# Three re-orderings in a hybrid diffusion trunk: the opening's products, weight cuts in the norm between layers, a convolution chunk

## The chip, the cores and the metric

The kernel runs on one core of one Trainium2 chip. The metric is the device time of one execution in microseconds (us); before the change it was 1175.28 (median of 3 runs, 1175.14 to 1176.17). The engines go by their names in the profile: PE (TensorE, matrix products; PEld its weight loads), DVE (VectorE), ACT (ScalarE), POOL (GpSimd), SP (SyncE, which issues most DMAs). Each runs its instructions in the order in which the program lists them, and waits for the others by semaphores.

## What is computed

Two layers over 512 tokens of width 1024, with a context of 256 tokens:

```python
for l in range(DEPTH):                                  # DEPTH = 2
    m = (sc_c @ w_mod[l] + b_mod[l])[:, None, :]        # sc_c = silu(c)
    sh1, s1, g1, sh2, s2, g2 = jnp.split(m, 6, axis=-1)
    h = modulate(rmsnorm(x, norm_g[l, 0]), sh1, s1)     # h * (1 + scale) + shift
    if l % 2 == 0:      # spatial gating beside neighbourhood attention
        hc = modulate(rmsnorm(ctx, norm_g[l, 0]), csh1, cs1)
        y, yc = even_mixer(h, hc, w_in[i], w_out[i], ...)
    else:               # gated projection, 31-tap convolution, layer norm, silu, projection
        y = conformer_conv(h, w_pw1[i], b_pw1[i], w_dw[i], ...)
    x = x + g1 * y
    x = x + g2 * sq_relu_mlp(modulate(rmsnorm(x, norm_g[l, 1]), sh2, s2), w_ff1[l], w_ff2[l])
return rmsnorm(x, final_g)
```

All is in float32.

## The kernel before

Activations lie transposed: channels on the 128 partitions, in 8 blocks k, tokens along the free axis (two halves of 256, a and b). A product in float32 accuracy is made of three matmuls: each operand is split into a high part (a cast, ACT, L93) and a low part (a subtraction on DVE or POOL, L94), and `mm3` (L88 to L90) issues high x high, weight's low x high, and high x operand's low. In `first_products` these are called hh, lh and hl. The order is written out by hand: the scheduler is off, every engine runs what the Python code emits, in that order.

Weights come in tiles of 1 MB (`raw`, two buffers) and are cut in four *pieces* each (`W.piece(i, q)`: cast on ACT, subtraction on DVE, or on POOL with `pool`, or on both by turns with "both"). The last piece of a tile issues the DMA of a later one. `W.pieces(n)` cuts the next n pieces where it stands in the code.

**Opening.** The first norm's factor: squares and sums (L383 to L393) give `dev`, `deviations()` (L405, four small products and a copy) spreads it to `r0`, `scaled(f)` multiplies two blocks of x by it. The modulation of layer 0 is made in four parts f: `mod_products(f)` (L421, twice four matmuls of 32 columns of weights `wmA`), a copy (ACT, L426), `next`, four transposes (L430), `next`, and three small DVE operations to shift and scale (L435 to L438). Then `first_operand(f)` makes the operand blocks k = 2f and 2f + 1 (hhi on ACT, L464; hlo on DVE, L465 and L466). `first_products(ks, ns)` multiplies them into four banks `q0`, of two weight tiles (n = 0, 1 and 2, 3). After f = 3 follow: a weight cut with POOL, the last first products (k = 6, 7), squares and additions over the context (ACT and DVE, L310 to L321), and their column sum on PE (`total`, L327).

**Norm between layers.** `norm_between` is called three times: ahead of layer 0's MLP (near 260 us), ahead of the convolution (610) and ahead of layer 1's MLP (800). It ends one projection and begins the next without a gap: output blocks 4 and 5 whole (`chunk`), 6 and 7 for token half a, then for half b. `residual`'s evacuation adds a block into x (DVE, L1012), squares it (ACT, L313) and adds the square *of the block before* (DVE, L321; `flush` adds the last one). `ss.total(a0, a1)` (flush, then L327) stands inside the products of block 6, half b; from it ACT and DVE make the factor (L331, L332), and `modulate`, one step of the generator for each k, makes t (DVE, L346), hhi (ACT) and hlo (DVE for even, POOL for odd k, one step later). The next layer's four products for half a (`together(four, ...)`) use these operands k by k; inside them stands the column sum of half b (L327 again).

**Convolution.** `glu(c)` makes the gated block c, and its evacuation (DVE, L1218) writes the padded row `ypad`; SP then issues DMAs that spread it into `y4` (16; for c = 7 only 10, the rest are ACT copies). `conv_pe(c, t0, t1)` runs the taps as 32-column matmuls on `y4` (L1262).

## Time and profile before

| | us |
|---|---|
| median of 3 runs | 1175.28 |
| profiled execution, its own time | 1176.03 |
| its span, first to last instruction | 1174.2 |
| PE busy (share of the span) | 1154.7 (98%) |
| DVE busy | 722.4 (62%) |
| ACT busy | 473.9 (40%) |
| POOL busy | 170.0 (14%) |

The profile's mean granted clock of PE is 0.996 of full speed. PE's busy time is near the whole span, so the places to read are those few where PE waited, which engine it waited for, and how near to waiting it was at the others.

### The profile page before, as it was taken

How to read it: one execution, taken by the hardware profiler on the slowest of the kernel's cores; microseconds unless marked ns; L12 is line 12 of the kernel's file. 1: busy time of each engine (PE TensorE's matmuls, PEld its weight loads, DVE VectorE, ACT ScalarE, POOL GpSimd, SP SyncE). 2: the span in 40 equal slices, each digit the busy share in tenths (PEclk: the TensorE clock that was granted, in tenths of full speed). 3: DMA queues.
4: the chain of work that ended last, by engine and by line, in shares of the span. 5: the costliest groups of instructions: out<-in, count | busy, mean ns of one | idle time of the engine just before them, and what ended most of it. 6: DMA issues, size and time to landing. Idle time of an engine off the chain costs nothing.

```text
span 1174.2 us, 16562 instructions
## 1 busy us (share of the span) xinstructions
PE 1154.7 (98%) x6620; PEld 959.6 (82%) x6620; DVE 722.4 (62%) x1252; ACT 473.9 (40%) x939; POOL 170.0 (14%) x162
## 2 busy tenths in 40 slices
PE   8999999999999999999999999999999999999997
PEld 4688898889888888888889666698988888888887
DVE  4765778758765665666666878577643443443445
ACT  4474455546431422423336233564632331341423
POOL 0250327533000000000023110143200000000001
PEclk9999999999999999999999999999999999999999
DMA  9624543351554554554541444303232332232322
GB/s 383 228 81 137 188 162 109 126 215 37 215 210 152 212 215 156 203 215 172 186 144 41 151 113 140 99 24 122 72 107 73 108 108 77 103 108 72 108 73 72
DMA packets 31469, 161.91 MB, mean 138 GB/s; under 512 B 4320, under 2 KB 7904, under 8 KB 15008
## 3 DMA queue, kind: packets, MB, share of 16 engines
q1 hardware_dynamic: 27360, 146.09, 35.6%
q10 hardware_dynamic: 4032, 14.76, 3.7%
q8 instruction: 52, 0.85, 0.3%
q14 instruction: 25, 0.20, 0.1%
HBM read 152.52 MB, written 2.10 MB: 132 GB/s over the span
## 4 chain that ended last, share of the span: by engine, by line
PE 87%; DVE 6%; DMA 3%; ACT 2%; issue 1%; POOL 0%; ACTq 0%; DVEq 0%; SPq 0%; POOLq 0%
PE ps L88 23%; PE ps L90 22%; PE ps L89 22%; PE ps L214 4%; PE ps L211 4%; PE ps L212 4%; PE ps L1262 3%; PE ps L892 1%; DMA graw<-in_wmA_dram 1%; DVE graw L557 1%; DMA graw<-in_wmB_dram 1%; PE ps L846 1%; DVE acc L321 1%; PE ps L421 1%; PE ps L876 1%
## 5 line engine op out<-in xcount | busy, mean ns | idle before, releaser
L93 ACT CAST whi<-raw 128x512 fp32r<-128x512 f32 x340 | 191.2, 616 | 199.4 <-PE ps L90 152.3
L88 PE MATMUL ps<-hhi,whi 128*128 128x512 f32 x640 | 251.6, 393 | 1.4 <-DVE gn L743 1.4
L90 PE MATMUL ps<-hlo,whi 128*128 128x512 f32 x640 | 249.3, 390 | 0.6 <-DVE hlo L466 0.6
L89 PE MATMUL ps<-hhi,wlo 128*128 128x512 f32 x640 | 249.4, 390 | 0.2 <-DVE wlo L94 0.2
L94 DVE TENSOR_TENSOR wlo<-raw,whi 128x512 fp32r<-128x512 f32 x284 | 194.7, 723 | 35.6 <-ACT whi L93 34.7
L90 PE MATMUL ps<-hid,whi 128*128 128x512 f32 (+1 forms) x520 | 196.3, 378 | 0.0
L89 PE MATMUL ps<-hid,wlo 128*128 128x512 f32 (+1 forms) x520 | 196.3, 378 | 0.0
L88 PE MATMUL ps<-hid,whi 128*128 128x512 f32 (+1 forms) x520 | 196.3, 378 | 0.0
L1012 DVE SCALAR_TENSOR_TENSOR x<-ps,mod,x 128x512 f32<-128x512 f32 (+1 forms) x94 | 62.7, 668 | 156.8 <-PE ps L90 147.8
L88 PEld LDWEIGHTS ps<-hhi,whi 128*128 128x128 f32 x640 | 120.1, 188 | 32.4 <-issue 5.3
L94 POOL TENSOR_TENSOR wlo<-raw,whi 128x512 fp32r<-128x512 f32 x56 | 81.6, 1473 | 426.9 <-ACT whi L93 426.8
L90 PEld LDWEIGHTS ps<-hlo,whi 128*128 128x128 f32 x640 | 120.1, 188 | 26.1 <-DVE hlo L466 1.0
L89 PEld LDWEIGHTS ps<-hhi,wlo 128*128 128x128 f32 x640 | 120.2, 188 | 24.5 <-DVE wlo L94 0.5
L557 DVE CUSTOM_DVE_ANT_0 graw<-graw,cB,vec 128x1024 f32<-128x1024 f32 x80 | 107.4, 1345 | 15.8 <-DMA graw<-in_wmB_dram 15.8
L88 PEld LDWEIGHTS ps<-hid,whi 128*128 128x128 f32 x520 | 97.8, 188 | 18.2
L89 PEld LDWEIGHTS ps<-hid,wlo 128*128 128x128 f32 x520 | 97.8, 188 | 18.1
L90 PEld LDWEIGHTS ps<-hid,whi 128*128 128x128 f32 x520 | 97.8, 188 | 18.1
L1138 DVE TENSOR_TENSOR z<-z 128x512 f32<-128x512 f32 (+1 forms) x72 | 46.1, 646 | 95.5 <-ACT z L1136 95.5
L1136 ACT ACTIVATE z<-ps 128x512 f32<-128x512 f32 (+1 forms) x72 | 38.9, 550 | 140.6 <-PE ps L90 137.1
L1142 DVE TENSOR_TENSOR hid<-z,hid 128x512 fp32r<-128x512 f32 (+1 forms) x72 | 45.7, 641 | 43.3 <-ACT hid L1140 43.3
L1140 ACT CAST hid<-z 128x512 fp32r<-128x512 f32 (+1 forms) x72 | 40.6, 572 | 51.4 <-DVE z L1138 51.4
L1492 POOL TENSOR_TENSOR o<-o,rstd 128x256 f32<-128x256 f32 x2 | 1.9, 950 | 323.1 <-DVE rstd L332 323.1
(261 smaller groups left out, 1695.4 us busy)
## 6 DMA issues: line engine op xcount, KB each, us to landing
raw<-in_w_ff_dram SPq DMA_DIRECT2D x64, 1024.0 KB
graw<-in_wmB_dram SPq DMA_DIRECT2D x28, 1024.0 KB
graw<-in_wmB_dram ACTq DMA_DIRECT2D x24, 512.0 KB
raw<-in_w_pw_dram SPq DMA_DIRECT2D x12, 1024.0 KB
raw<-in_w_in_dram SPq DMA_DIRECT2D x10, 1024.0 KB
wmA<-in_wmA_dram SPq DMA_DIRECT2D x6, 1024.0 KB
y<-ypad SPq DMA_DIRECT2D x90, 67.5 KB
raw<-in_w_out_dram SPq DMA_DIRECT2D x4, 1024.0 KB
```

Source lines behind the costliest of these rows:

```text
L88: pe.matmul(ps, w[0], a[0], start=first, stop=False)
L89: pe.matmul(ps, w[1], a[0], start=False, stop=False)
L90: pe.matmul(ps, w[0], a[1], start=False, stop=last)
L93: (e or act.copy)(hi, src)
L94: (el or dve).tensor_tensor(lo, src, hi.bitcast(F32), op=ALU.subtract)
L211: pe.matmul(ps, w[0][:, k, c : c + P], a[0], start=n == 0, stop=False)
L212: pe.matmul(ps, w[1][:, k, c : c + P], a[0], start=False, stop=False)
L214: pe.matmul(ps, w[0][:, k, c : c + P], a[1], start=False, stop=n == len(ks) - 1)
L557: dve.tensor_tensor_reduce(out=wv, in0=wv, in1=cB, scale=1.0, scalar=vcol(V_BMOD, l * 48 + q * 8 + j % 8), op0=ALU.mult, op1=ALU.add, accu ...
L1012: dve.scalar_tensor_tensor(x[:, m, t0:t1], ps, gate[:, m : m + 1], x[:, m, t0:t1], op0=ALU.mult, op1=ALU.add)
L1138: dve.tensor_tensor(z, z, z, op=ALU.mult)
L1142: dve.tensor_tensor(lo, z, hi.bitcast(F32), op=ALU.subtract)
```

## The change

Opening: `deviations()` and `scaled(0)` stand ahead of the first modulation products; a 128-column warm-up product is gone; each later `scaled(f + 1)` stands behind the weight's pieces; the first products can be called by parts (all hh, then all lh, and hl later), and are spread differently around the modulation's products, which now run as blocks of eight. Norm: no pieces ahead of block 6's evacuation; one piece behind it, one behind block 7's, and two behind block 6's evacuation for half b, all four with the subtraction on DVE (before: three ahead of the evacuation, two of them on DVE and one on POOL, and a fourth on POOL). Convolution: the first half of conv 5 stands behind `glu(7)`.

```diff
+    def first_products(ks, ns=range(4), parts=("hh", "lh", "hl")):
+
+        for part in parts if len(parts) < 3 else [None]:
+            for k in ks:
+                for n in ns:
+                    w, c = wqk[n // 2], (n % 2) * P
+                    for i, j in [("hl".index(e) for e in pt) for pt in (parts if part is None else (part,))]:
+                        pe.matmul(q0[n], w[i][:, k, c : c + P], h[k][j], start=k == i == j == 0,
+                                  stop=k == KC - 1 and j == 1)
...
-        if f < 3:
-            scaled(f + 1)
-
+
+    deviations()
+    scaled(0)
     pm = mod_products(0)
     next(pm)
-    deviations()
-    scaled(0)
     next(pm)
     pbs = [silu_rows(0)]
-    keep_warm(1, 128)
     next(pm)
...
     W.piece(0, 0)
+    wqk = {0: W.his[0]}
     first_operand(0)
+    first_products((0, 1), (0, 1), ("hh", "lh"))
     for q in range(1, 4):
         W.piece(0, q)
+    W.use()
...
-    wqk = {0: W.use()}
-    first_products((0, 1), (0, 1))
+    scaled(1)
     pm = mod_products(1)
     next(pm)
     next(pm)
+    first_products((0, 1), (0, 1), ("hl",))
     next(pm)
+    run(pm)
     W.piece(1, 0)
-    run(pm)
+    wqk[1] = W.his[1]
     first_operand(1)
+    first_products((0, 1), (2, 3), ("hh", "hl"))
+    first_products((0, 1), (2, 3), ("lh",))
     for q in range(1, 4):
         W.piece(1, q)
+    W.use()
+    scaled(2)
...
-    wqk[1] = W.use()
-    first_products((0, 1), (2, 3))
+    first_products((2,), (0, 1))
     pm = mod_products(2)
     next(pm)
-    first_products((2,), (0, 1))
     next(pm)
-    first_products((2,), (2,))
+    first_products((3,), (0, 1))
+    next(pm)
     run(pm)
     first_operand(2)
-    first_products((2,), (3,))
-    first_products((3,), (0, 1))
+    scaled(3)
+    first_products((2, 3), (2, 3))
+    first_products((4,))
     pm = mod_products(3)
     next(pm)
-    first_products((3,), (2,))
     next(pm)
-    first_products((3,), (3,))
+    first_products((5,), (0, 1))
+    next(pm)
     run(pm)
     first_operand(3)
-    first_products((4,))
-    first_products((5,))
+    first_products((5,), (2, 3))
...
-        chunk(6, w, 0, acts, evac, 0, ks, a0, a1, 3, "both")
+        chunk(6, w, 0, acts, evac, 0, ks, a0, a1, 0)
+        W.pieces(1)
         seven = together([(7, w, P)], acts, evac, a0, a1, ks)[0]
         seven()
-        W.pieces(1, pool)
+        W.pieces(1)
...
         go(ma_)
         six()
         go(ma_)
+        W.pieces(1)
         seven = together([(7, w, P)], acts, evac, b0, b1, ks)[0]
+        W.pieces(1)
         W.free()
...
         glu(6)
         conv_pe(4)
         conv_weights(6)
-        conv_pe(5, a0, a1)
         take(4)
         glu(7)
         preload(AF.Silu)
         work(100)
+        conv_pe(5, a0, a1)
         conv_pe(5, b0, b1)
```

On PE around the opening's fourth transposes (L430 of `kon`), before; `ps_196` to `ps_199` are the four banks `q0`, `hhi_186` is block k = 3, `hhi_188` k = 4:

```order
L90 MATMUL ps_198<-hlo_187,whi_286 128x512
L421 MATMUL ps_375<-wmA_107,sc_115 32x512 x4
L88 MATMUL ps_199<-hhi_186,whi_286 128x512
L89 MATMUL ps_199<-hhi_186,wlo_287 128x512
L90 MATMUL ps_199<-hlo_187,whi_286 128x512
L430 MATMUL ps_392<-kon,ms_387 128x128 x4
L88 MATMUL ps_196<-hhi_188,whi_236 128x512
L89 MATMUL ps_196<-hhi_188,wlo_237 128x512
```

and after, where `hhi_190` is k = 5 and `hhi_192` k = 6 (the operand that these transposes lead to):

```order
L421 MATMUL ps_392<-wmA_105,sc_115 32x512 x4
L421 MATMUL ps_392<-wmA_107,sc_115 32x512 x4
L457 MATMUL ps_196<-hhi_190,whi_235 128x512
...
L457 MATMUL ps_197<-hlo_191,whi_235 128x512
L430 MATMUL ps_409<-kon,ms_401 128x128 x4
L457 MATMUL ps_198<-hhi_190,whi_290 128x512
...
L457 MATMUL ps_199<-hlo_191,whi_290 128x512
L457 MATMUL ps_196<-hhi_192,whi_235 128x512
```

The transposes stood behind k = 3 and stand behind half of k = 5: 48 products ahead of them before, 66 after, and 6 instead of 24 between them and block k = 6.

On DVE at the first norm, from block 6's evacuation on, before (`x<-ps` an evacuation, `acc` the sum of squares, `t` the operand's product, `hlo_2622` the low part of k = 0):

```order
L94 TENSOR_TENSOR wlo_2753<-raw_2672,whi_2752 128x512 x2
L1012 SCALAR_TENSOR_TENSOR x<-ps_2727,mod_433,x 128x256
L321 TENSOR_TENSOR acc_2540<-acc_2540,sq_2722 128x512
L1012 SCALAR_TENSOR_TENSOR x<-ps_2764,mod_433,x 128x256
L321 TENSOR_TENSOR acc_2540<-acc_2540,sq_2761 128x256
L321 TENSOR_TENSOR acc_2540<-acc_2540,sq_2790 128x256
L332 RECIPROCAL rstd_2816<-rstd_2816 128x256
...
L359 SCALAR_TENSOR_TENSOR hlo_2622<-t_2828,mod_434,hhi_2621 128x256
L346 SCALAR_TENSOR_TENSOR t_2864<-x,gs_2725,rstd_2816 128x256
```

and after:

```order
L1020 SCALAR_TENSOR_TENSOR x<-ps_2726,mod_432,x 128x256
L321 TENSOR_TENSOR acc_2539<-acc_2539,sq_2721 128x512
L94 TENSOR_TENSOR wlo_2756<-raw_2671,whi_2755 128x512
L1020 SCALAR_TENSOR_TENSOR x<-ps_2759,mod_432,x 128x256
L321 TENSOR_TENSOR acc_2539<-acc_2539,sq_2752 128x256
L94 TENSOR_TENSOR wlo_2756<-raw_2671,whi_2755 128x512
L321 TENSOR_TENSOR acc_2539<-acc_2539,sq_2785 128x256
L332 RECIPROCAL rstd_2809<-rstd_2809 128x256
...
L359 SCALAR_TENSOR_TENSOR hlo_2621<-t_2821,mod_433,hhi_2620 128x256
L94 TENSOR_TENSOR wlo_2756<-raw_2671,whi_2755 128x512 x2
L346 SCALAR_TENSOR_TENSOR t_2863<-x,gs_2724,rstd_2809 128x256
```

A subtraction (`wlo`) now stands between the last two additions, and two between the low part of k = 0 and the product t of k = 2.

On ACT at the same place, before:

```order
L313 ACTIVATE sq_2761<-x 128x256
L313 ACTIVATE sq_2790<-x 128x256
L93 CAST whi_2752<-raw_2672 128x512
L331 ACTIVATE rstd_2816<-ps_2814,epsc 128x256
...
L349 CAST hhi_2623<-t_2834 128x256
L351 ACTIVATE hhi_2625<-t_2864,mod_434 128x256
```

and after:

```order
L313 ACTIVATE sq_2752<-x 128x256
L93 CAST whi_2755<-raw_2671 128x512
L313 ACTIVATE sq_2785<-x 128x256
L93 CAST whi_2755<-raw_2671 128x512
L331 ACTIVATE rstd_2809<-ps_2807,epsc 128x256
...
L349 CAST hhi_2622<-t_2827 128x256
L93 CAST whi_2755<-raw_2671 128x512 x2
L351 ACTIVATE hhi_2624<-t_2863,mod_433 128x256
```

Two casts moved from ahead of the squares to a place between the operands of k = 1 and k = 2.

## Rows read from the trace of the kernel before

**Rows 1.** The page, part 1: busy time and share of each engine

```profile
PE 1154.7 (98%) x6620; PEld 959.6 (82%) x6620; DVE 722.4 (62%) x1252; ACT 473.9 (40%) x939; POOL 170.0 (14%) x162
```

**Rows 2.** Waits of PE, whole span: total us, times, longest us

```profile
PE ps L327 <- DVE acc L321: 2.6, 2, 1.8
PE ps L1262 <- DMA y<-ypad: 1.5, 2, 0.8
PE ps L88 <- DVE gn L743: 1.4, 1, 1.4
```

**Rows 3.** Timeline, opening: start us, us, engine line, out<-in, count [idle before <-releaser]

```profile
14.96 1.06 PE L421 MATMUL ps<-graw,sc 128*32 128x512 f32 x8 [1.19 <-DMA graw<-in_wmA_dram]
...
19.22 0.60 PE L430 MATMUL ps<-kon,ms 128*128 128x128 f32 x4
...
25.15 1.92 PE L421 MATMUL ps<-wmA,sc 128*32 128x512 f32 x16
...
42.49 0.64 PE L430 MATMUL ps<-kon,ms 128*128 128x128 f32 x4
...
46.17 0.39 PE L90 MATMUL ps<-hlo,whi 128*128 128x512 f32 x1
46.39 0.39 PE L88 MATMUL ps<-hhi,whi 128*128 128x512 f32 x1
```

**Rows 4.** Timeline, end of the opening: last operand half, column sum

```profile
47.51 1.67 DVE L466 TENSOR_TENSOR hlo<-x,hhi 128x512 fp32r<-128x512 f32 x1
...
54.85 0.67 PE L327 MATMUL ps<-acc,ones 128*128 128x256 f32 x2 [0.81 <-DVE acc L321]
```

**Rows 5.** Windows: us, busy (instructions) of PE PEld DVE ACT POOL, PEclk, DMA

```profile
193.60:199.00 5.40, 3.66 (x18) 2.59 (x16) 5.26 (x16) 2.31 (x6) 2.66 (x2) 1.00 0.36 134
807.40:810.70 3.30, 3.30 (x16) 3.21 (x16) 2.35 (x3) 0.55 (x2) 0.83 (x1) 0.50 0.44 112
```

**Rows 6.** Timeline, first norm: DVE, ACT and PE

```profile
261.18 0.69 DVE L94 TENSOR_TENSOR wlo<-raw,whi 128x512 fp32r<-128x512 f32 x1 [0.53 <-ACT whi L93]
262.22 1.42 DVE L94 TENSOR_TENSOR wlo<-raw,whi 128x512 fp32r<-128x512 f32 x1 [0.34 <-ACT whi L93]
...
265.38 0.99 DVE L321 TENSOR_TENSOR acc<-acc,sq 128x256 f32<-128x256 f32 x2
...
265.82 0.60 ACT L93 CAST whi<-raw 128x512 fp32r<-128x512 f32 x1
...
266.57 0.60 PE L327 MATMUL ps<-acc,ones 128*128 128x256 f32 x2
...
271.09 0.87 DVE L346 SCALAR_TENSOR_TENSOR t<-x,gs,rstd 128x256 f32<-128x256 f32 x2
...
271.41 0.41 ACT L349 CAST hhi<-t 128x256 fp32r<-128x256 f32 x1
271.72 0.51 ACT L351 ACTIVATE hhi<-t,mod 128x256 fp32r<-128x256 f32 x1
...
273.83 0.28 PE L211 MATMUL ps<-hhi,w 128*128 128x256 f32 x1
...
275.60 0.42 DVE L321 TENSOR_TENSOR acc<-acc,sq 128x256 f32<-128x256 f32 x1
...
276.71 0.38 PE L327 MATMUL ps<-acc,ones 128*128 128x256 f32 x1
```

**Rows 7.** Timeline, second and third norm: column sums, and the casts' DMA

```profile
617.69 0.70 PE L327 MATMUL ps<-acc,ones 128*128 128x256 f32 x2
...
801.42 1.66 ACT L93 CAST whi<-raw 128x512 fp32r<-128x512 f32 x3 [1.50 <-DMA raw<-in_w_ff_dram]
...
806.88 0.82 PE L327 MATMUL ps<-acc,ones 128*128 128x256 f32 x2 [1.76 <-DVE acc L321]
```

**Rows 8.** Timeline, convolution on DVE: sums behind conv 5, evacuation of block 7

```profile
727.09 0.69 DVE L1286 TENSOR_TENSOR lsum<-lsum,sq 128x512 f32<-128x512 f32 x1 [1.13 <-ACT sq L1284]
...
737.19 0.75 DVE L1218 SCALAR_TENSOR_TENSOR ypad<-ps,vec,sg 128x512 f32<-128x512 f32 x1 [1.38 <-PE ps L90]
```

More of the change, by code (lines that the diff above doesn't have):

```diff
@@ L448, in body @@
     q0 = [bank() for _ in range(4)]
-    def first_products(ks, ns=range(4)):
-        for k in ks:
-            for n in ns:
-                w, c = wqk[n // 2], (n % 2) * P
-                mm3(q0[n], (w[0][:, k, c : c + P], w[1][:, k, c : c + P]), h[k], k == 0, k == KC - 1)
+    def first_products(ks, ns=range(4), parts=("hh", "lh", "hl")):
[6 more added lines that the diff above has]
+                                  stop=k == KC - 1 and j == 1)
     def scaled(f):
```

## The prediction

> **What bounds the kernel now.** I read the page first: TensorE (PE) is busy for 98% of the span [rows 1], so a change can give back only the few microseconds in which PE waits, and costs whatever it adds to them. Next the waits of PE: 2.6 us for a column sum at L327, 1.5 us, in two pieces, for DMAs of the convolution's operand at L1262, and a 1.4 us wait in the mixer [rows 2]. Then the stretches around the three edits: the timeline of the opening [rows 3, 4], the granted clock after a wait [rows 5], and the engines' timelines at the norm between layers [rows 6, 7] and at the convolution [rows 8]. To be seen there: in the opening PE waits little but its fourth set of modulation transposes starts a chain on other engines that ends in L327; in the norm, L327 waits at one of three places and comes within 0.2 us of it at the others; in the convolution PE waits for copies that start too late.
>
> **The opening.** Up to the fourth transposes (L430) it is a list of PE work with few waits, so I count it. PE stands idle for 1.19 us before the first modulation products (start 14.96) [rows 3]; the deviations' four small products, which stood between its two halves, move into that hole, and the eight products behind them run as one block of 1.9 us (25.15 [rows 3]); the small warm-up product goes. That brings the first transposes from 19.22 to about 18.25. The first eight products by parts need neither second-half operand, so the second modulation's products start at about 22.7 instead of 25.15 and the second transposes at 25.5. From there PE has a full list: a product takes 0.228 us (46.17 to 46.39 [rows 3]), a modulation block 1.9 us, the transposes 0.4 of their 0.64 us until the next product starts, and I add 0.1 us for each change between them. Third transposes: 25.5 + 0.4 + 18 products 4.2 + block 1.9 + six products 1.5 = 33.5. Fourth: 33.5 + 0.4 + 24 products 5.6 + block 1.9 + six products 1.5 = 42.9, against 42.49 [rows 3]. So the gain of the start is used up: 66 products now stand ahead of the fourth transposes where 48 stood, 18 x 0.228 = 4.1 us, and the waits removed are slightly less. What hangs on the fourth transposes is unchanged on each engine: the last operand halves, cuts of a weight on ScalarE and GpSimd, eight squares and seven additions; it takes 54.85 - 42.49 = 12.36 us to L327 [rows 3, 4]. So L327 goes from 54.85 to about 55.3: **+0.4 us** (bounds -0.5 and +1.0: a microsecond of the list counted wrongly either way).
>
> PE, however, now has less to do meanwhile: the last operand half ends at 47.51 + 1.67 = 49.2, 6.7 us after the transposes [rows 4], so at 49.6 in the new order, and ten products follow it: 52.0. From there to 55.3 PE idles 3.2 us, where it idled 0.81 us [rows 4]. At 806.88 a wait of 1.76 us was followed by a stretch at clock 0.50 (1.2 GHz), in which PE issued 16 products of 256 columns in 3.3 us [rows 5, 7], where 29 would fit by half of the 0.228 us; after the mixer's wait of 1.4 us the clock stayed at 1.00 (2.4 GHz) [rows 2, 5]. A wait of 3.2 us lies beyond the longer one, so I take such a stretch here: half of 3.3 us, **+1.6 us** (bounds 0 and two such stretches, 3.3).
>
> **The norm between layers, three places.** Take the first. The column sum's last addition follows the square of the second evacuation (ScalarE; the cast at 265.82 stands right behind it); the two additions end at 265.38 + 0.99 = 266.37, and PE reaches L327 at 266.57 without a wait [rows 6]. In the new order ScalarE does square, cast, and VectorE does the weight's subtraction *before* that addition: cast ends 265.82 + 0.60 = 266.42, subtraction 0.69 (the 261.18 row) to 267.1, addition 0.4 to 267.5. L327 at 267.5: +0.95. Then the second pair of pieces. Row 271.41 is the cast that ends the second operand; both new casts follow it on ScalarE (from 271.7, 0.6 each), VectorE waits for the first, subtracts twice and only then makes the third operand's product t, which stood at 271.09 [rows 6]. Counted from L327: casts to 5.8 and 6.3 us, subtractions to 6.5 and 7.2, t at 7.2 instead of 4.5, operand ready at 8.3 instead of 5.7. PE wants it 273.83 - 266.57 = 7.26 us after L327 [rows 6]: a wait of 1.05 us. VectorE stays 2.7 us late, while the additions for the second L327 end 9.45 us after the first in the old order and PE comes there 276.71 - 266.57 = 10.14 us after it [rows 6]: now 12.0 against 11.2, 0.75 us more. The first place costs 0.95 + 1.05 + 0.75 = **+2.7 us**. The second place has the same steps with L327 at 617.69 [rows 7] and 0.8 in place of 0.95: **+2.5 us**. The cover that VectorE had for two of these subtractions was GpSimd; it is gone.
>
> At the third place the casts ahead of the evacuation waited 1.50 us for their weight's DMA [rows 7], both evacuations came late, L327 waited 1.76 us and the slow clock followed. In the new order the evacuations pass the late weight; L327 comes, by the steps above, about 1.0 us earlier (805.9), the wait is 0.9 us, shorter than the 1.4 us that left the clock alone, and 1.6 us of slow clock goes. The two later waits, 1.75 us, come here too: -1.0 - 1.6 + 1.75 = **-0.8 us**. Norm in all: **+4.4 us** (bounds: without the later waits, -0.9; with each of them half as long again, +7).
>
> By the Trainium skill, "SBUF — State Buffer", section "Who interferes with whom", VectorE and GpSimd share a port pair as an exclusive lock, and the loser blocks for the other's whole instruction. The subtraction at 262.22 took 1.42 us, twice its own 0.69, while GpSimd ran its piece [rows 6]: the trace agrees. By that rule the third subtraction, which starts during GpSimd's half of the second operand, would end 0.3 us later at each place, 0.9 us in all, and the sum would be 1181.1; and taking pieces from GpSimd would speed VectorE's neighbours, here only where nobody waits for them.
>
> **The convolution.** glu(7) now starts 3.4 us earlier on PE. Its evacuation at 737.19 had waited 1.38 us for PE with VectorE free [rows 8]; VectorE itself is freed 1.1 us sooner, since the square behind conv 5 (727.09, waited 1.13) no longer waits. So the evacuation comes 2.5 us earlier, and the ten DMAs with it. PE reaches conv 7 when it did, so both its waits go [rows 2]: **-1.5 us** (bounds -2.0, with the restarts behind them, and -0.5, where the last DMA is still late). Behind it stand VectorE's statistics, which move with PE.
>
> **The sum.** +0.4 + 1.6 + 2.7 + 2.5 - 0.8 - 1.5 = +4.9 us. The profiled execution took 1176.03 us, its span 1174.2 and 1.83 around it, and lies 0.75 above the median of the runs; 1174.2 + 4.9 + 1.83 - 0.75 = 1180.2.
>
> **Rivals.** (a) The clock holds in the opening: all else stands, 1178.6. Against it: the idle time is nearly twice the one that was followed by a slow stretch. (b) Both later waits in the norm stay away, because the weight's last pieces fit into idle time of ScalarE and VectorE: norm -0.9, and the opening's clock holds: 0.4 - 0.9 - 1.5 = -2.0, 1173.3. It decides at 1.6 us: so late may the third operand be (272.23 to 273.83); I count 2.7. (c) Faster: what the change removes is gone and nothing comes instead. The second and third transposes are 2.3 to 2.6 us early; were the fourth so too, L327 would come 2.5 earlier, the norm's third place gives 1.8 + 1.6, the first two cost nothing, conv 1.5: -7.4, 1167.9. For it: every wait that it names is in the trace. Against it: the 18 products ahead of the fourth transposes and the subtraction ahead of the last addition stand in the order. (d) Worse: two slow stretches in the opening (+1.7) and conv's DMAs still late (+1.5): 1183.4.
>
> **How the numbers follow.** Forecast 0.40, (a) 0.13, (b) 0.28, (c) 0.10, (d) 0.09. Slower by over 0.2% (2.35 us, about what a measurement of this kernel can tell from no change) are the forecast, (a) and (d): 0.62. (b) lies at the edge: 0.20 of it within 0.2%, 0.08 faster; with (c) faster is 0.18. The range 1172.9 to 1183.4 reaches from (b), with its edge towards faster, to (d) and leaves out (c) and the tails, 2 in 10.
>
> **What would show it.** In the changed kernel's waits: L327 in the opening with some 3 us and clock 0.5 behind it; L327 at all three norms with about 0.9 us for the sum, and a wait of about 1 us of the products for the third operand; no wait at conv 7; the fourth transposes at 42.9. Wrong it is if the fourth transposes come before 41, or if PE meets the third operand without a wait.

## The result, and the profile after

The changed kernel took 1180.97 us (median of 5 runs, 1180.73 to 1182.18) where the kernel before took 1175.28: a ratio of 1.0048, 95% interval 1.0034 to 1.0063. It is slower by 5.7 us (4.0 to 7.4). The profiled execution took 1181.01 us with a span of 1179.2. The two profiled executions differ by 4.98 us and not by 5.7, because the one of the kernel before lies 0.75 us above its median. One execution of a later run (the filled wait, below) took 1933.31 us at a mean granted clock of 0.557 and is left out of that run's figures.

PE's busy time and the three longest sums of its waits, which answer to [rows 1, 2] (total us, times, longest us):

```profile
PE 1155.6 (98%) x6618; PEld 960.0 (81%) x6618; DVE 724.9 (61%) x1258; ACT 473.9 (40%) x939; POOL 163.0 (14%) x156
...
PE ps L327 <- DVE acc L321: 6.8, 7, 3.0
PE ps L211 <- ACT hhi L351: 2.6, 3, 0.9
PE ps L88 <- DVE gn L751: 1.4, 1, 1.4
```

L327 waits at seven places instead of two; a group that was not there before (L211 for hhi, three times) has come, and the convolution's wait for ypad has gone.

The opening, answering to [rows 3, 4]: PE's fourth transposes and column sum in the timeline (start us, us, then the idle time before and its releaser), and below them the window of 3.41 us that follows (busy time of PE, PEld, DVE, ACT, POOL, then the granted clock):

```profile
42.97 0.60 PE L430 MATMUL ps<-kon,ms 128*128 128x128 f32 x4
...
55.28 0.67 PE L327 MATMUL ps<-acc,ones 128*128 128x256 f32 x2 [3.05 <-DVE acc L321]
...
56.39:59.80 3.41, 3.41 (x10) 2.63 (x9) 3.09 (x5) 1.04 (x3) 0.00 (x0) 0.50 0.24 82
```

The first norm, answering to [rows 6]: timeline of DVE, ACT and PE:

```profile
268.51 0.28 PE L214 MATMUL ps<-ylo,whi 128*128 128x256 f32 x1
268.51 0.69 DVE L94 TENSOR_TENSOR wlo<-raw,whi 128x512 fp32r<-128x512 f32 x1 [0.66 <-ACT whi L93]
269.12 0.42 DVE L321 TENSOR_TENSOR acc<-acc,sq 128x256 f32<-128x256 f32 x1
...
269.59 0.70 PE L327 MATMUL ps<-acc,ones 128*128 128x256 f32 x2 [0.80 <-DVE acc L321]
...
275.49 1.41 DVE L94 TENSOR_TENSOR wlo<-raw,whi 128x512 fp32r<-128x512 f32 x2 [1.20 <-ACT whi L93]
...
276.82 0.87 DVE L346 SCALAR_TENSOR_TENSOR t<-x,gs,rstd 128x256 f32<-128x256 f32 x2
...
277.95 0.39 PE L211 MATMUL ps<-hhi,w 128*128 128x256 f32 x1 [0.84 <-ACT hhi L351]
...
281.06 0.42 DVE L321 TENSOR_TENSOR acc<-acc,sq 128x256 f32<-128x256 f32 x1
...
281.53 0.70 PE L327 MATMUL ps<-acc,ones 128*128 128x256 f32 x2 [0.45 <-DVE acc L321]
```

The subtraction (L94) stands ahead of the last addition (L321), and L327 waits for it; two more subtractions, which themselves wait 1.20 us for their cast, stand ahead of the third operand's t (L346), and L211 waits. The second norm repeats this with 0.80, 0.84 and 0.39 us. At the third [rows 7] the wait ahead of L327 is half of what it was:

```profile
811.44 0.70 PE L327 MATMUL ps<-acc,ones 128*128 128x256 f32 x2 [0.86 <-DVE acc L321]
```

Block 7's evacuation in the convolution, answering to [rows 8], starts without a wait:

```profile
742.05 0.74 DVE L1229 SCALAR_TENSOR_TENSOR ypad<-ps,vec,sg 128x512 f32<-128x512 f32 x1
```

PE was 7.36 us behind the kernel before at the second norm's end, so this is 734.7 in the time of before, 2.5 us earlier than 737.19.

How far PE was behind the kernel before at each column sum, and what the places between them cost, from the two traces (one execution of each kernel):

| place | after minus before at its end, us | the place's share | forecast |
|---|---|---|---|
| opening's L327 | +0.44 | +0.44 | +0.4 |
| to the first norm's L327, its 0.80 taken off | +2.22 | +1.78 | +1.6 |
| first norm, second L327 | +4.82 | +2.60 | +2.7 |
| second norm, second L327 | +7.36 | +2.54 | +2.5 |
| convolution, to the third norm's L327 without its wait | +5.46 | -1.90 | -1.5 |
| third norm, second L327 | +4.81 | -0.65 | -0.8 |
| end of the span | +4.98 | +0.17 | 0 |

### The profile page after: what moved, and what is told of

It reads as the page before. It is cut to its first block, busy times and chain, and to the rows that moved or that the text cites. A ratio compares the mean times of both kernels' runs of the same rounds, so it can differ in the third digit from the quotient of the medians.

```text
span 1179.2 us, 16552 instructions
## 1 busy us (share of the span) xinstructions
PE 1155.6 (98%) x6618; PEld 960.0 (81%) x6618; DVE 724.9 (61%) x1258; ACT 473.9 (40%) x939; POOL 163.0 (14%) x156
## 4 chain that ended last, share of the span: by engine, by line
PE 88%; DVE 7%; ACT 3%; DMA 1%; issue 1%; ACTq 0%; DVEq 0%; POOL 0%; POOLq 0%
PE ps L88 23%; PE ps L89 22%; PE ps L90 22%; PE ps L1273 3%; PE ps L214 3%; PE ps L211 3%; PE ps L212 3%; PE ps L457 1%; PE ps L900 1%; PE ps L376 1%; DVE graw L565 1%; DMA graw<-in_wmB_dram 1%; PE ps L854 1%; DVE acc L321 1%; PE ps L421 1%
## 5 line engine op out<-in xcount | busy, mean ns | idle before, releaser
L88 PE MATMUL ps<-hhi,whi 128*128 128x512 f32 x608 | 238.6, 392 | 1.4 <-DVE gn L751 1.4
L89 PE MATMUL ps<-hhi,wlo 128*128 128x512 f32 x608 | 237.0, 390 | 0.0
L90 PE MATMUL ps<-hlo,whi 128*128 128x512 f32 x608 | 236.9, 390 | 0.0
L94 DVE TENSOR_TENSOR wlo<-raw,whi 128x512 fp32r<-128x512 f32 x290 | 196.8, 716 | 36.5 <-ACT whi L93 35.6
L88 PEld LDWEIGHTS ps<-hhi,whi 128*128 128x128 f32 x608 | 114.2, 188 | 28.2 <-issue 3.2
L90 PEld LDWEIGHTS ps<-hlo,whi 128*128 128x128 f32 x608 | 114.2, 188 | 23.8
L89 PEld LDWEIGHTS ps<-hhi,wlo 128*128 128x128 f32 x608 | 114.3, 188 | 22.9
L94 POOL TENSOR_TENSOR wlo<-raw,whi 128x512 fp32r<-128x512 f32 x50 | 74.5, 1506 | 409.6 <-ACT whi L93 409.5
L1147 ACT ACTIVATE z<-ps 128x512 f32<-128x512 f32 (+1 forms) x72 | 38.9, 550 | 136.9 <-PE ps L90 135.3
L313 ACT ACTIVATE sq<-x 128x256 f32<-128x256 f32 (+1 forms) x41 | 20.3, 496 | 67.0 <-DVE x L1020 66.7
```

The source lines that it names most:

```text
L88: pe.matmul(ps, w[0], a[0], start=first, stop=False)
L89: pe.matmul(ps, w[1], a[0], start=False, stop=False)
L90: pe.matmul(ps, w[0], a[1], start=False, stop=last)
L94: (el or dve).tensor_tensor(lo, src, hi.bitcast(F32), op=ALU.subtract)
L1147: act.activation(z, ps, AF.Relu)
```

## The experiments

There were twelve runs of 4 to 12 executions each. Beside each of three groups of them the kernel before ran again, 70 times in all, with medians of 1175.39 to 1175.55 us; the ratios are to these. A comparison holds an effect of one or two microseconds only loosely: the way from the opening's L327 to the first norm's (the mixer), with PE's wait at its end and any stretch at the slow clock taken off, took between 211.5 and 213.4 us in the profiled executions, whatever the kernel. So the time says whether a part costs or gains, and the trace of each says where.

### Each part alone

The three parts of the change's diff were put into the kernel before one by one.

**The opening alone.** It ran twice.

> The kernel before with the change's opening alone. My theory: the fourth transposes start at 42.9 to 43.0 instead of 42.49, L327 at 55.3 instead of 54.85 (+0.4), PE waits 3.0 us there, and a stretch at clock 0.50 of some 3.4 us follows (+1.6): +2.1 us against the kernel before, 1177.4. Rival one, that the time comes from elsewhere and the clock's stretch takes the place of one that the kernel before has later: the wait and the stretch are there, but a later wait shrinks by as much, +0.4 or less. Rival two, that the earlier second and third transposes help: the fourth would be 2.5 us early, -2.5 us.

> The kernel before with the change's opening alone, a second time, since its first time (1175.37) lay 2 us under what its trace has in the opening. If the time is truly unchanged: within 0.1% of the kernel before again, L327 in the opening with its wait of 3.0 us and the third norm's wait or its stretch of the clock smaller than 1.76 us and 1.6 us. If the first time was chance: 1176.5 to 1177.5.

Measured: 1175.37 us (ratio 1.0002, 0.9994 to 1.0011) and 1175.11 (0.9995, 0.9986 to 1.0004): no change, where I expected 2 us more. In both traces the opening loses as forecast (L327 at 55.77 and 55.13, waits of 3.04 and 3.00 us, the slow clock behind them). It comes back at the third norm. Timeline and windows of the second of these kernels:

```profile
55.13 1.19 PE L327 MATMUL ps<-acc,ones 128*128 128x256 f32 x2 [3.00 <-DVE acc L321]
...
807.49 0.70 PE L327 MATMUL ps<-acc,ones 128*128 128x256 f32 x2 [0.70 <-DVE acc L321]
...
807.50:810.80 3.30, 3.30 (x26) 3.25 (x27) 1.97 (x2) 0.47 (x1) 1.28 (x1) 1.00 0.30 62
```

L327 waits 0.70 us there (0.51 in the first of them) where it waited 1.76 [rows 7], and the clock behind it stays at 1.00 where it was 0.50 [rows 5]: 1.1 to 1.25 and 1.5 us back. Rival one of the first expectation holds. What was seen together with the shorter wait stands at the end of this document.

**The norm alone.**

> The kernel before with the change's four weight pieces in the norm alone. My theory: each place loses at three points: 0.8 to 0.95 us at L327, 0.85 to 1.05 us at the products for the third operand, 0.45 to 0.75 us at the second L327; at the third place 1.0 us and a stretch at clock 0.50 worth 1.6 us are won first. +2.6 +2.6 -0.8 = +4.4 us, 1179.7. Rival, that the pieces fit into idle time of ScalarE and VectorE: no wait for the third operand and none at the second L327, -0.9 us in all, 1174.4.

Measured: 1181.07 us, ratio 1.0056 (1.0041 to 1.0071), 5.6 us more. L327 waits 0.80, 0.80 and 0.86 us, the third operand's products 0.84, 0.84 and 0.90, the second L327 0.46, 0.40 and 0.46, as in the changed kernel. This part alone is as slow as the whole change, and it cost 1.2 us more than I expected. In the profiled execution the slow stretch is gone from the third norm, but one stands in the convolution, behind two waits that the kernel before has too (there 0.84 and 0.64 us, and the clock held). This execution was the slowest of the six (1183.09 us), and by their mean clock the others need not have had a stretch, so it does not account for the 1.2 us; what may is said under the slow clock below. Timeline and window:

```profile
751.31 0.59 PE L1265 MATMUL ps<-y,cB 128*32 128x256 f32 x2 [1.42 <-DMA y<-ypad]
752.52 5.12 PE L1265 MATMUL ps<-y,cB 128*32 128x256 f32 x58 [0.62 <-DMA y<-ypad]
...
752.90:756.10 3.20, 3.20 (x39) 2.05 (x32) 1.94 (x5) 0.48 (x2) 0.00 (x0) 0.53 0.42 110
```

**The convolution alone.**

> The kernel before with the first half of conv 5 behind glu(7) alone. My theory: both waits of L1262 for ypad's DMAs (0.84 and 0.64 us) go: -1.5 us, as far as -2.0 with the restarts behind them, 1173.3 to 1173.8. Rival, that the last DMA stays late: -0.5 us, 1174.8. Rival two, that VectorE's statistics behind it take the gain back at the third norm: 0, with a longer wait of L327 there.

Measured: 1174.32 us, ratio 0.999 (0.998 to 1.0001), 1.1 us less, at the edge of what can be told. The trace has no wait for ypad. At the third norm, L327 waits a little longer than before, and the clock holds all the same:

```profile
807.34 0.70 PE L327 MATMUL ps<-acc,ones 128*128 128x256 f32 x2 [2.03 <-DVE acc L321]
...
807.40:810.70 3.30, 3.30 (x26) 3.25 (x27) 2.02 (x2) 0.47 (x1) 1.28 (x1) 1.00 0.34 65
```

The three parts give 0 (-0.1 and -0.3 by the medians), +5.6 and -1.1: +4.5, within the interval of the whole.

### Is the slow clock the price of the opening's wait?

```diff
+    warm = [1]
+    WARM = 6
...
             self.ps = bank()[:, : t1 - t0]
+            if warm:
+                warm.pop()
+                for _ in range(WARM):
+                    pe.matmul(self.ps, ones, ones.unsqueeze(1).to_broadcast([P, 2, P]), start=True, stop=True)
             pe.matmul(self.ps, ones, self.acc[:, t0:t1], start=True, stop=True)
```

> The changed kernel with six products of ones (256 columns, float32, 0.43 us each, as the warm-up at L376 takes) added ahead of the opening's L327, into the bank that L327 then overwrites; they fill 2.6 of the 3.05 us in which PE waited there. L327 itself stays at 55.3, since DVE's additions set it. My theory, that the wait is what lets the clock fall: the clock stays at 1.00 behind L327, PE issues at full pitch from the start, -1.6 us against the changed kernel, 1179.4. Rival, that the stretch at 0.50 comes from something else at this place (the work behind it, or how busy PE was long before): the stretch stays, 0 us, 1181.0. With either, a stretch may come back at the third norm, where the wait is 0.86 us in the changed kernel; I expect none there.

Measured: 1181.50 us (1.0060, 1.0042 to 1.0078), no less than the changed kernel's 1180.97. The trace does what I expected of it at this place; timeline and window (L334 is L327 here, L333 the added products):

```profile
52.22 2.75 PE L333 MATMUL ps<-ones 128*128 128x256 f32 x12
55.33 0.70 PE L334 MATMUL ps<-acc,ones 128*128 128x256 f32 x2 [0.36 <-DVE acc L324]
...
56.40:59.80 3.40, 3.40 (x17) 2.78 (x16) 3.01 (x4) 1.06 (x3) 0.00 (x0) 1.00 0.26 89
```

L327 starts when it did, and PE issues 17 products where it issued 10. With the wait filled the clock held. One execution does not prove that the filling did it, since the next run kept its clock with the wait left as it was.

The other executions say more, since the record has the mean granted clock of each. In the fourteen profiled ones it was 0.996 or 0.997 with a slow stretch and 0.997 or 0.998 without, so 0.996 or less points to a stretch and 0.997 tells nothing. Of the five kernels whose L327 waits 3.0 us or more in the opening, 21 of 47 executions had 0.996 or less (three of five of the changed kernel). With the wait filled it was none of 5; with the wait cut to 0.83 us (`transposes_early`, below) none of 12 (eight at 0.997 and four at 0.998, which took 1176.5 us alike); and with no wait there, in the two kernels with the mended opening, none of 9. `sums_early`, where PE waits 1.62 us for an operand instead, has it in three of 5. So, as far as these counts go, the wait is what brings the stretch, in about half of the executions. The kernel before, which waits 0.81 us there and 1.76 us at the third norm, had 0.996 or less in 24 of its 70 executions. That may be why the norm alone cost more than I expected: I had counted the 1.6 us of clock at the third norm as won in full.

What a stretch is worth at the end is known roughly: those 24 executions took 1176.3 us on average, and 30 at 0.998 took 1174.8. That filling the wait saves time is not shown: in the profiled execution PE waited 1.4 us instead of 0.6 for VectorE in the mixer (L861 for gn), and 0.6 us for ypad in the convolution, where the changed kernel did not.

### The norm: which of the pieces costs what

**The addition ahead of the piece.**

```diff
         seven()
+        ss.flush()
         W.pieces(1)
```

> The changed kernel with one line more in the norm: the last addition for L327 (the flush) is emitted ahead of the second weight piece instead of behind it. My theory, that the subtraction (0.69 us) ahead of the addition is the whole of the wait at L327: the waits of 0.80, 0.80 and 0.86 us at L327 go, the subtraction runs while L327 and the square root (0.48 us, L331) run, so the reciprocal (L332) is not later for it; all behind it moves 0.8 us forward, -2.4 us against the changed kernel, 1178.6. Rival, that the subtraction then stands ahead of the reciprocal and costs the same there: L327's waits go, the wait for the third operand grows by 0.7 to about 1.6 us, 0 in all.

Measured: 1178.34 us, ratio 1.0023 (1.0014 to 1.0031), 2.6 us under the changed kernel. Timeline of the first norm, DVE and PE:

```profile
267.08 0.42 DVE L321 TENSOR_TENSOR acc<-acc,sq 128x256 f32<-128x256 f32 x1
267.59 0.69 DVE L94 TENSOR_TENSOR wlo<-raw,whi 128x512 fp32r<-128x512 f32 x1
267.71 0.60 PE L327 MATMUL ps<-acc,ones 128*128 128x256 f32 x2
...
275.97 0.39 PE L211 MATMUL ps<-hhi,w 128*128 128x256 f32 x1 [0.84 <-ACT hhi L351]
```

All three waits of L327 are gone, and the later ones are as they were (0.84 and 0.45 us), so the subtraction costs nothing behind the addition: it runs beside L327 and the square root. My theory holds, with its number.

The same trace takes something from the opening's term. Its opening is that of the changed kernel:

```profile
56.16 0.67 PE L327 MATMUL ps<-acc,ones 128*128 128x256 f32 x2 [3.05 <-DVE acc L321]
...
57.00:60.40 3.40, 3.40 (x17) 2.79 (x16) 2.81 (x4) 1.06 (x3) 0.00 (x0) 1.00 0.27 94
```

The wait is the same to 0.01 us, and no slow stretch follows in this execution, here or anywhere before the end.

**One late piece instead of two.**

```diff
         chunk(6, w, 0, acts, evac, 0, ks, a0, a1, 0)
-        W.pieces(1)
+        W.pieces(2)
...
         seven = together([(7, w, P)], acts, evac, b0, b1, ks)[0]
-        W.pieces(1)
         W.free()
```

> The changed kernel with one of the two late weight pieces of the norm moved behind block 6's evacuation for half a (two pieces there, one behind block 7's, one late). My theory, that two casts and two subtractions make the third operand 2.7 us late where PE allows some 1.8: with one, it is 1.35 us late, and the waits of 0.87 us for the third operand and of 0.43 us at the second L327 both go at all three places, while L327 keeps its 0.80: -3.9 us, 1177.1. Rival one, that the wait comes from the one piece that is left (ScalarE's order, whatever its length): half of it stays, -1.5 to -2. Rival two, that the second early subtraction (ending about 266.95 where block 7's evacuation starts at 267.03) delays that evacuation: L327 waits 1.2 to 1.5 us instead of 0.8, -2 or less.

Measured: 1179.51 us, ratio 1.0032 (1.0022 to 1.0042), 1.5 us under the changed kernel, not 3.9. Timeline of the first norm, with GpSimd's half of the second operand:

```profile
275.17 0.74 POOL L357 TENSOR_TENSOR hlo<-t,hhi 128x256 fp32r<-128x256 f32 x1 [13.67 <-ACT hhi L349]
275.64 0.81 DVE L94 TENSOR_TENSOR wlo<-raw,whi 128x512 fp32r<-128x512 f32 x1 [1.20 <-ACT whi L93]
...
277.51 0.38 PE L211 MATMUL ps<-hhi,w 128*128 128x256 f32 x1 [0.25 <-ACT hhi L351]
...
281.09 0.70 PE L327 MATMUL ps<-acc,ones 128*128 128x256 f32 x2 [0.45 <-DVE acc L321]
```

Two of my numbers fell. A single late piece makes the third operand not 1.35 but 2.0 us late: VectorE first stands still for 1.20 us, because the piece's cast is queued on ScalarE behind the second operand's, and then subtracts for 0.81; the second piece adds only 0.6. So the wait of 0.84 us shrinks to 0.25 and does not go. And the second L327 waits 0.45 us as before. From the start of t for the third operand to the end of the last addition VectorE takes 281.06 + 0.42 - 276.82 = 4.66 us in the changed kernel and the same here (276.38 to 281.04); PE, from the third operand's first product to this L327, takes 3.13 us without the wait in both. Both run from the same operand. So in both kernels, with waits of 0.84 and of 0.25 us for that operand, the same 0.45 us follow.

### The opening: what L327 hangs on

**The products behind the transposes.**

```diff
-    first_products((2, 3), (2, 3))
-    first_products((4,))
+    first_products((2, 3), (2,))
     pm = mod_products(3)
     next(pm)
     next(pm)
-    first_products((5,), (0, 1))
+    first_products((2, 3), (3,))
     next(pm)
     run(pm)
     first_operand(3)
-    first_products((5,), (2, 3))
+    first_products((4, 5))
```

> The changed kernel with 18 of the products that stand ahead of the opening's fourth modulation block moved behind its transposes (six stay ahead of the block, six between it and the transposes). My theory, that those 18 are why L327 comes late: the fourth transposes start 4.1 us earlier, at 38.9; L327 could start 12.3 us later, at 51.2, and PE, which has the same list of products, comes there at 51.4 to 52.2: its wait falls from 3.05 to at most 0.5 us and no stretch at clock 0.50 follows. L327 3.1 to 3.9 us earlier and 1.6 of clock: -4.7 to -5.5 us by the trace, 1175.5 to 1176.3. Rival, that the chain behind the transposes is held by something else (the context's DMA, the weight's, ScalarE's cuts): the transposes come early, L327 stays at 54 or later, 0 to -1.3 us.

Measured: 1176.48 us, ratio 1.0007 (0.9998 to 1.0015), 4.5 us under the changed kernel, where 4.7 to 5.5 were expected. L327 still waits 0.83 us, more than the 0.5 that I had allowed. Timeline of PE:

```profile
39.61 0.60 PE L430 MATMUL ps<-kon,ms 128*128 128x128 f32 x4
...
51.94 0.67 PE L327 MATMUL ps<-acc,ones 128*128 128x256 f32 x2 [0.83 <-DVE acc L321]
```

From the fourth transposes to L327 it is 12.33 us, where it was 12.36 in the kernel before [rows 3, 4] and 12.31 in the changed one: three places in the program, one chain. (The first transposes start 0.76 us later than in the changed kernel's profile; without that, 38.85, where 38.9 was expected.)

**The sums off the chain.** Four squares with their additions stand ahead of the fourth modulation block, four behind its copy.

```diff
     scaled(3)
+    cs = SumSq()
+    for k in range(4):
+        cs.add(ctile[k], 0, TC)
     first_products((2, 3), (2, 3))
     first_products((4,))
     pm = mod_products(3)
     next(pm)
     next(pm)
+    for k in range(4, KC):
+        cs.add(ctile[k], 0, TC)
     first_products((5,), (0, 1))
...
-    cs = SumSq()
-    for k in range(KC):
-        cs.add(ctile[k], 0, TC)
     cs.total(0, TC)
```

> The changed kernel with the eight squares and seven additions over the context, which stood behind the opening's last weight cuts, emitted around the fourth modulation block: four ahead of it, four behind its copy. The transposes stay where they are. My theory, that L327 waits only because its sum hangs on the end of that chain: L327 waits for nothing and starts when PE's products end, at 52.2 instead of 55.28, no stretch at clock 0.50 follows, and what the sums take from VectorE (0.5 us each, seven) delays the last operand by 0.5 us at most: -3.0 -1.6 +0.5 = -4.1 us, 1176.9. Rival, that the squares wait for the context's DMA and hold the copy and the operands behind them on ScalarE: the fourth transposes at 44 or later, and PE waits for the last operand's halves instead, -1 us or less.

Measured: 1180.19 us, ratio 1.0036 (1.0023 to 1.0048), 0.8 us under the changed kernel and not to be told from it. Timeline of ACT, DVE and PE:

```profile
41.91 0.42 ACT L310 ACTIVATE acc<-ctx 128x256 f32<-128x256 f32 x1 [4.56 <-DMA ctx<-in_ctxT_dram]
...
44.13 2.02 DVE L321 TENSOR_TENSOR acc<-acc,sq 128x256 f32<-128x256 f32 x4 [0.52 <-ACT sq L313]
46.07 0.18 DVE L435 TENSOR_REDUCE modA<-ps 128x8 f32<-128x32 f32 x1
...
47.55 0.50 PE L457 MATMUL ps<-hhi,whi 128*128 128x512 f32 x1 [1.62 <-ACT hhi L468]
...
54.52 0.59 PE L327 MATMUL ps<-acc,ones 128*128 128x256 f32 x2
```

L327 waits for nothing, as my theory has it; but the squares stand on ScalarE until the context's DMA lands, and their additions on VectorE now stand ahead of the modulation's last steps (L435 to L438): L435 starts at 46.07, 2.1 us behind the fourth transposes, where in the changed kernel it was 0.6 us. PE waits 1.62 us for the last operand instead. The rival had this wait, but by another step: the fourth transposes did not come late (43.94, as far behind the first ones as in the changed kernel). The wait was moved, for the most part, not removed.

### Mended, part by part and together

In the norm, two pieces stand behind block 6's evacuation, then the flush and two more behind block 7's, and none later. In the opening, the products stand behind the transposes as above, and `W.pieces(4, pool)` stands behind the squares and additions over the context. `best` has both and the changed convolution; the other two have one part each, in the kernel before. The edits, against the changed kernel:

```diff
         chunk(6, w, 0, acts, evac, 0, ks, a0, a1, 0)
-        W.pieces(1)
+        W.pieces(2)
         seven = together([(7, w, P)], acts, evac, a0, a1, ks)[0]
         seven()
-        W.pieces(1)
+        ss.flush()
+        W.pieces(2)
...
-        W.pieces(1)
         seven = together([(7, w, P)], acts, evac, b0, b1, ks)[0]
-        W.pieces(1)
```

```diff
-    W.pieces(4, pool)
     first_products((6, 7))
     cs = SumSq()
     for k in range(KC):
         cs.add(ctile[k], 0, TC)
+    W.pieces(4, pool)
     cs.total(0, TC)
```

> The kernel before with the norm's four pieces placed as in the run best (two behind block 6's evacuation, flush, two behind it), its opening and convolution as they were. My theory, that the change's loss in the norm is the order of pieces and additions and not the place behind the evacuations: the first two places cost 0 (no wait of L327, third operand on time, no wait at the second L327), the third gains the wait of 1.76 us and what the clock loses behind it: -1.8 to -3.4 us, 1172 to 1173.7. Rival, that four subtractions on VectorE are too many wherever they stand: a wait of 0.4 us or more at the second L327 of each place, and 1174 or later.

Measured: 1172.67 us, ratio 0.9978 (0.9969 to 0.9987), 2.7 us under the kernel before. No wait at any of the three places. Four subtractions on VectorE are not too many; where they stand decides.

> The kernel before with the opening as in the run best, norm and convolution as they were. My theory: L327 without a wait at some 51.3 instead of 54.85, -3.6 us, which the mixer passes on; the third norm keeps its wait. 1171.8. Rival, that a later wait takes it back, the mixer's for VectorE (L88 for gn) or the third norm's for a weight whose DMA comes no earlier: 1173.5 or later, with that wait longer by as much.

Measured: 1169.0 us, ratio 0.9943 (0.993 to 0.9957), 6.4 us under the kernel before, more than the 3.6 expected. L327 starts at 50.35 without a wait, 4.5 us earlier; and the third norm gives again what it gave to the opening alone, a wait of 0.80 us instead of 1.76 and a clock that holds.

> The changed kernel with three edits: 18 products moved behind the opening's fourth transposes; the opening's last weight cuts behind the squares and additions over the context; in the norm two weight pieces behind block 6's evacuation, then the flush, two pieces behind it, and none later. My theory: L327 in the opening without a wait at some 51.3 (54.85 in the kernel before), no wait of L327 or of the third operand at any of the three places, none of L1262 for ypad worth more than 0.8 us. Against the kernel before: -3.6 in the opening, 0 at the first two norms, -1.5 in the convolution, up to -3.4 at the third norm (its wait of 1.76 and the clock behind it): 1166.9 to 1170.4. Rival one, that the two subtractions behind the flush delay the reciprocal: 0.6 us at each place, 1.8 more. Rival two, that the mixer waits for work on VectorE and GpSimd that starts no earlier: the opening's gain is gone by the first norm, 1170.5 to 1174.

Measured: 1166.91 us, ratio 0.9921 (0.9907 to 0.9935): 8.5 us under the kernel before and 14 under the changed one. Timeline of PE:

```profile
38.65 0.60 PE L430 MATMUL ps<-kon,ms 128*128 128x128 f32 x4
...
50.00 0.59 PE L327 MATMUL ps<-acc,ones 128*128 128x256 f32 x2
...
261.51 0.60 PE L327 MATMUL ps<-acc,ones 128*128 128x256 f32 x2
...
798.16 0.61 PE L327 MATMUL ps<-acc,ones 128*128 128x256 f32 x2
```

None of these waits. L327 stands 4.8 us earlier than in the kernel before in the opening, 8.7 at the third norm, and 10.3 behind the clock's stretch that the kernel before has there. The mixer passes the opening's gain on; neither rival came.

## Why the prediction was right, point by point

**The opening, +0.4.** Right in its steps: the second, third and fourth transposes were forecast at 25.5, 33.5 and 42.9 and stand at 25.55, 33.58 and 42.97, L327 at 55.3 and 55.28. That L327 came to 0.02 us is partly luck, since in the six profiled executions with this opening as it is, or with its wait filled, it stands between 55.13 and 56.16. That the 18 products ahead of the transposes are the cause, and that a chain of 12.36 us hangs on the transposes, is shown by moving the products: both moved together.

**The clock behind it, +1.6.** In the profiled execution the stretch came, and the executions' clocks show that the wait brings it, but in about half of them. As a term of the sum it was too certain, and so was its counterpart, the 1.6 us that the forecast won back at the third norm: in the sum the two cancel, so that the total would have come out the same without the clock. That the sum is right is luck as far as the clock goes, and so is the table's +1.78, which is one pair of executions on a way that by itself varies by 1.9 us. The same wait of 3.0 to 3.05 us was followed by the stretch in four profiled executions (the changed kernel, twice the opening alone, one late piece) and not in a fifth. The opening alone left the time where it was, because the third norm gave back as much: the forecast added the opening and the norm as if neither touched the other. In the changed kernel there was less to give back: the third norm's wait of 0.86 us is that of the piece ahead of the addition there, as `add_first` shows.

**The norm, +2.7 and +2.5.** Measured +2.60 and +2.54, and the norm alone costs 5.6 us in time, nearly the whole loss. The first wait was forecast at 0.95 and 0.8 and is 0.80 at both; the second at 1.05 and is 0.84; the third at 0.75 and is 0.45 and 0.39. So the waits come out shorter than forecast, all but one. But the forecast reckoned in starts of instructions, and in starts the first place is as it said: L327 comes 0.96 us later behind the product ahead of it than in the kernel before (1.08 against 0.12 us; 0.95 forecast), the third operand's first product 1.10 later behind L327 (277.95 - 269.59 = 8.36 against 7.26; 1.05 forecast), and the second L327 0.70 later behind that product (0.75 forecast). The rest of each is the pause that a wait leaves between PE's products beyond what the profile counts as idle. (The table's 2.60 counts 0.80 of the first; the other 0.16 is in the row above it.) The first wait is shown by one line that takes it away. The third loss is set by where two chains from the third operand end: the forecast had VectorE's last addition 12.0 us behind L327 and PE there at 11.2, and they were at 11.9 and 11.5. What was wrong is my expectation for `late_pieces`, that this wait would go when VectorE is less late: PE is less late with it.

**The third norm, -0.8.** Measured -0.65. In the profile the forecast's parts came: a wait of 0.86 instead of 1.76 us, a clock that holds, and the two later waits. But it leaned on one execution's wait of 1.76 us and one execution's stretch, and with another opening that wait is 0.5 to 0.8 us in the old order, too.

**The convolution, -1.5.** Measured -1.90 in the trace and -1.1 us in the time of this part alone. The evacuation came 2.5 us earlier, as forecast. Its waits for ypad come to 0 to 0.8 us in the eight profiled executions with the new order and to 0.5 to 2.0 in the six with the old one, so what it gains differs from execution to execution by as much as the forecast's bounds.

**VectorE beside GpSimd.** By the rule of the Trainium skill, "SBUF — State Buffer", section "Who interferes with whom", that one of the two engines blocks for the whole of the other's instruction, the third subtraction would have ended 0.3 us later at each place, by the forecast's estimate. The row of the kernel with one late piece has one such subtraction by itself: 0.81 us beside GpSimd's half of the second operand, against 0.69 for the same form elsewhere. The trace agrees with the rule in kind and not in size: by these rows the two overlap for 0.27 us, and the subtraction loses 0.12.

**The rivals.** (a), the clock holds, is what at least two of the changed kernel's five executions did, by their mean clock of 0.998. (b), the weight's pieces fit into idle time, is false for these positions and true for the mended ones. (c) is what the mended opening brings, and it needs the fourth transposes early, as it said. Nothing of (d) was seen in the changed kernel: one stretch in the opening, no wait for ypad.

## What to carry to other kernels

Ask of every step that moves which instruction of the same engine now stands behind it and who waits for that one: a subtraction of 0.69 us cost 0.80 ahead of an addition and nothing behind it. An instruction that must wait for another engine costs that wait too: the first late piece cost 2.0 us, the second 0.6. Where an early start is wanted, move the work behind the step on which the long chain hangs; and since a wait for late data gives back what an earlier place has lost, parts that are measured alone need not add up.

## What the runs showed of the hardware

**Length alone does not tell whether the clock falls behind a wait.** In the profiled executions it fell behind 1.76 us [rows 5, 7] and not behind 2.03 at the same place; behind 3.05 us in one kernel and not behind 3.05 in another; and twice behind shorter ones in the convolution (1.42 and 0.62 us with the norm alone, 1.30 and 0.61 with the norm mended). Seven of the fourteen profiled executions had one stretch of 3.4 us at 0.50 before the end, and seven had none. Nor does the fall stand at a fixed distance from the wait: in the four executions with 3 us it came between 0.1 us ahead of the wait's end and 1.4 us behind it. What decides was not settled.

**A transfer of instructions beside a weight's load.** In the kernel before, the casts ahead of the third norm's L327 wait for a weight of 1 MB [rows 7]. From its issue on SP to its last packet this load took 5.3 to 6.2 us in the four kernels with the old opening, and 4.3 to 4.6 in the ten with a new one, with the old order of the norm and the convolution or the new one. Within 4.1 us of the issue, the DMA view of the kernel before has this row (packets, MB, share of 16 engines) beside the load's own, and so have the three others with the old opening; in four with a new one (the changed kernel, the opening alone, and the mended one alone and in `best`) it is not there, and the 16 KB of instructions start 4.1 to 4.2 us behind the issue:

```profile
q8 instruction: 1, 0.02, 1.5%
```

And on SP, the wait of the next issue for this load, in the kernel before and with the opening alone (second time):

```profile
SPq L120 <- DMA raw<-in_w_ff_dram: 1.2, 1, 1.2
```

```profile
SPq L120 <- DMA raw<-in_w_ff_dram: 0.2, 1, 0.2
```

That an edit to the opening shifts this transfer some 750 us later, and that it is what makes the load late, fits all fourteen traces, but no run moved the transfer by itself: it is a finding of things seen together, not shown.
